# The opening of a hybrid attention step as one list by positions in the products: early loads of x, rows of x in other places, first roots on ScalarE and VectorE

## The chip, the cores and the metric

The kernel runs on one core of one Trainium2 chip. The metric is device time in microseconds (us) of one launch. The core has five engines with queues of their own: TensorE (PE), VectorE (DVE), ScalarE (ACT), GpSimd (POOL) and SyncE (SP), which here issues the DMAs. They meet through semaphores.

## The reference

One layer of a streaming encoder for a prompt of 1024 tokens (8 blocks of 128) and a sample of 64 tokens that shares the weights. Cut to what matters here:

```python
h = rms_norm(x, g)
p = h @ w_in                         # [q_A k_A v_A | q_B k_B v_B | forget logits]
qa, ka = rms_norm(heads(q_A), g_qa), rms_norm(heads(k_A), g_ka)
logf = log_sigmoid(f_logit + b_f)
# attention A: chunks of 64 frames see themselves and 8 chunks before, 8 heads of 64
logits = q @ k.T * scale + rel_bias
o = softmax(where(mask, logits, -inf)) @ v
# attention B: forgetting attention, 8 heads; then
x += concat(o_A, o_B) @ w_o          # then memory cross-attention and a conv FFN
```

## The kernel before

The projection and the attention run in eight head pairs (p = 0 to 7; 0 to 3 are attention A). A pair takes its 384 columns of the weights (392 in the first, which has the forget columns too) and forms the product of each token block t with them into one PSUM bank, `pj`. All operands are split into a high and a low part (`whi`, `wlo`, `xhi`, `xlo`), and a product has three terms for each of eight k: 24 matmuls, in 8 *pieces* of three. x comes from memory transposed, in columns of 256 tokens (columns 0 to 3, each in two halves of four k); ACT makes the high part and DVE the low one. The rows of x (`xn`, a block of 128 tokens) are loaded a second time untransposed, to form each token's mean square on ACT (`stats`).

This case is about the *opening*, the first pair. The products of t = 0 to 3 are formed together while weights and x still arrive (`quad`, banks `tq`, `O` and two of `PT`); then t = 4 to 7 one by one; then the product of the sample's 64 tokens (`proj_sample`, 16 matmuls). Beside them runs the attention of the pair, in steps:

- `E(t)`: evicts a product from PSUM (copy of q and k, squares, values, forget column `flog`).
- `QA(n)`: for blocks 2n and 2n+1, ACT squares and copies, DVE reduces the squares (L369), adds a constant (L370), and POOL takes the power −1/2 (L371).
- `Z(t)`: norm of q and k: POOL multiplies by the roots (L375 for t < 4; `qk_norm` with L296 to L310 after that), DVE splits the values (L397, L398).
- `R(t)`: the *turn*: PE transposes q and k of four heads (L405) into bank `tq`, ACT makes `kh` and `q` (L319), DVE `kl` and the low half of `q` (L320).
- `U(n, j)`: scores of one head (unit n = 2 · group + head; a group is two blocks, j the block in it): matmuls into `S` (L578), DVE adds the bias and takes the row maximum (L581), ACT the exponential with its sum (L583), DVE the reciprocal (L584), POOL scales (L586). `S` is one tile of two banks.
- `V(n)`: values: PE transposes the weights of attention into `PT` (L618), ACT and DVE split them (`pth`, `ptl`, L619 and L620), PE sums (L633).

A list `opening[t]` holds the steps beside product t, and `weave` spreads them evenly between its pieces. Until the end of t = 5 all engines keep the order of the code (`ramp` marks it, and `in_order` adds the dependencies); after that a scheduler may change it, but for the splits. Units 5 to 7, and the turn of block 7, are left to the second pair.

```python
def weave(main, subs):
    j = 0
    for x, f in enumerate(main):
        f()
        while j * len(main) < len(subs) * (x + 1):
            subs[j]()
            j += 1
```

Of the kernel before, what the change touches and what calls it, by code (L numbers as in the profile page):

```python
# [41 lines left out]
def hybrid_step(ctx: ExitStack, tc: tile.TileContext, i: dict, o: dict):  # L42
# [76 lines left out]
    xs = xp.tile([P, KT, 2, S], F32R, name="xs")  # L119
# [16 lines left out]
    def split_x(hi, lo, raw, k):  # L136
        act.activation(hi, raw, ACT.Copy, scale=gcol[:, 0, k:k + 1])
        dve.scalar_tensor_tensor(lo, raw, gcol[:, 0, k:k + 1], f32(hi), op0=ALU.mult, op1=ALU.subtract)
# [12 lines left out]
    def load_stats(t):  # L151
        rows = P if t < NT else S
        xn = xns[t] = wk.tile([P, N], F32, name="s", bufs=4)
        nc.sync.dma_start(xn[:rows, :D], i["xn"][t * P:t * P + rows])
# [25 lines left out]
    def split_col(c, k, raw):  # L180
# [3 lines left out]
        split_x(*[x_part(a, k, c * 256, 256) for a in range(2)], raw, k)  # L184
# [4 lines left out]
    def sample_columns(raw):  # L189
# [4 lines left out]
        def split():  # L194
            act.copy(xs[:, :, 0], raw)
            dve.tensor_tensor(xs[:, :, 1], raw, f32(xs[:, :, 0]), op=ALU.subtract)
# [12 lines left out]
    for k in range(KT):  # L209
# [31 lines left out]
    def stats4():  # L241
        st = bank("pj")[:, :8].rearrange("p (t z) -> p t z", z=2)
        for t in range(4):
            pe.matmul(st[:, t], quads[0][:, 0, t * P:t * P + P], two, start=True, stop=True)
        ms = wk.tile([P, 9], F32, name="ms1", bufs=2)
        dve.tensor_scalar(ms[:, :4], st[:, :, 0], EPS, None, op0=ALU.add)
        rsq(wk, ms[:, :4], rstd1[:, 0:4], 4)
        dve.tensor_scalar(eps1[:, 0:4], ms[:, :4], EPS, None, op0=ALU.mult)

# [107 lines left out]
    sq4, raw4, r8 = [], [], {}  # L357

    def quad_norm(n):
        if not n:  # L360
            for x in (sq4, raw4):
                x.append(wk.tile([P, N], F32, name="s", bufs=4)[:, :1024].rearrange("p (t c) -> p t c", t=4))
        for t in range(2 * n, 2 * n + 2):
            act.activation(sq4[0][:, t], quad[t][:, 0:256], ACT.Square, scale=0.125)
            act.copy(raw4[0][:, t], quad[t][:, 0:256])
        m = wa.tile([P, 2, 4], F32, name="m8", bufs=2)
        r = r8[n] = wa.tile([P, 2, 4], F32, name="r8", bufs=2)
        c = slice(2 * n, 2 * n + 2)
        dve.tensor_reduce(m.rearrange("p t h -> p (t h)"), sq4[0][:, c].rearrange("p t (h d) -> p (t h) d", h=4), axis=AX.X, op=ALU.add)  # L369
        dve.tensor_tensor(m, m, eps1[:, c].rearrange("p (t o) -> p t o", o=1).broadcast_to([P, 2, 4]), op=ALU.add)  # L370
        pool.tensor_tensor(r, m, mhalf[:, 0:4].rearrange("p (o h) -> p o h", o=1).broadcast_to([P, 2, 4]), op=ALU.pow)  # L371

    def quad_qk(t):
# [3 lines left out]
        return qk, None  # L377

    def proj(p, t, pj, first=False):
# [4 lines left out]
        if not first:  # L384
            raw = wa.tile([P, 256], F32, name="qkraw", bufs=2)
            act.copy(raw, pj[:, 0:256])
            sq = squares(pj[:, 0:256], P)
        vf = wa.tile([P, 2, 64], F32, name="vf", bufs=2)
        act.activation(vf.rearrange("p h d -> p (h d)"), pj[:, 256:384], ACT.Copy, scale=rstd1[:, t:t + 1])
        if p == 0:  # L390
            dve.scalar_tensor_tensor(flog[:, t], pj[:, 384:392], rstd1[:, t:t + 1], bfb, op0=ALU.mult, op1=ALU.add)
# [1667 lines left out]
```

## Time and profile before

| | |
|---|---|
| median of 3 runs | 1751.9 us (1751.48 to 1755.92) |
| the profiled execution | 1751.61 us, span 1749.8 us |
| mean granted clock of PE | 0.995 |
| PE busy | 1700.0 us, 97% of the span |
| from 20 to 40 us | PE busy 15.84 of 20 us, clock 1.00 |
| from 40 to 60 us | PE busy 14.60 of 20 us, clock 0.83 |
| from 60 to 80 us | PE busy 16.27 of 20 us, clock 0.74 |
| from 80 to 100 us | PE busy 17.25 of 20 us, clock 1.00 |

The profile is of one execution. Busy time counts instructions that run; PE's matmuls are pipelined, so that a busy PE is not always PE at its peak. In a row of the timeline the first number is the start, the second the length, and the bracket at its end holds the idle time ahead of it on that engine and the instruction that ended it. In a row of waits stand the sum, the count and the longest. In a row of a group stand the busy time, the mean of one in ns, and the idle time ahead.

### The profile page before, as it was taken

How to read it: one execution, taken by the hardware profiler on the slowest of the kernel's cores; microseconds unless marked ns; L12 is line 12 of the kernel's file. 1: busy time of each engine (PE TensorE's matmuls, PEld its weight loads, DVE VectorE, ACT ScalarE, POOL GpSimd, SP SyncE). 2: the span in 40 equal slices, each digit the busy share in tenths (PEclk: the TensorE clock that was granted, in tenths of full speed). 3: DMA queues.
4: the chain of work that ended last, by engine and by line, in shares of the span. 5: the costliest groups of instructions: out<-in, count | busy, mean ns of one | idle time of the engine just before them, and what ended most of it. 6: DMA issues, size and time to landing. Idle time of an engine off the chain costs nothing.

```text
span 1749.8 us, 33690 instructions
## 1 busy us (share of the span) xinstructions
PE 1700.0 (97%) x12384; PEld 1653.9 (95%) x12384; DVE 1187.9 (68%) x2610; ACT 920.5 (53%) x2027; POOL 592.3 (34%) x874
## 2 busy tenths in 40 slices
PE   8898999999999999999999999999999999999999
PEld 7788999999998888999999999999999999999999
DVE  6778667677677755334444389777777777659996
ACT  6656667677677657334555455333334343434442
POOL 2646557779777302543443521000000000000000
PEclk9899999999999999999999999999999999999999
DMA  6222122222232677531112752222222222793332
GB/s 209 75 53 61 52 76 67 62 74 59 63 104 91 195 226 224 172 114 39 49 49 80 208 182 80 95 83 75 75 74 75 75 75 75 267 331 120 113 105 88
DMA packets 135156, 191.97 MB, mean 110 GB/s; under 512 B 23288, under 2 KB 78200, under 8 KB 134992
## 3 DMA queue, kind: packets, MB, share of 16 engines
q1 hardware_dynamic: 134992, 189.83, 34.6%
q8 instruction: 97, 1.59, 0.4%
q14 instruction: 67, 0.55, 0.1%
HBM read 148.01 MB, written 43.34 MB: 109 GB/s over the span
## 4 chain that ended last, share of the span: by engine, by line
PE 46%; DVE 5%; issue 2%; ACT 1%; POOL 1%; DMA 1%; SPq 0%; DVEq 0%; ACTq 0%; POOLq 0%
PE W L1614 26%; PE W L1938 10%; PE pj L1068 7%; PE S L1357 1%; PE tq L1393 1%; PE O L1393 1%; POOL lo L1050 1%; DVE f L1479 1%; PE PT L1380 0%; DVE lo L1479 0%; DVE lo L1050 0%; ACT hi L1478 0%; PE O L1357 0%; DMA f<-x2d 0%; DMA raw<-in_w_down_dram 0%
## 5 line engine op out<-in xcount | busy, mean ns | idle before, releaser
L353 PE MATMUL pj<-whi,xhi 128*128 128x384 f32 (+1 forms) x480 | 181.8, 379 | 0.4 <-ACT whi L131 0.4
L353 PE MATMUL pj<-wlo,xhi 128*128 128x384 f32 (+1 forms) x480 | 164.5, 343 | 5.4 <-POOL wlo L133 4.3
L353 PE MATMUL pj<-whi,xlo 128*128 128x384 f32 (+1 forms) x480 | 163.1, 340 | 0.0
L1614 PE MATMUL W<-h,hi 128*128 128x272 f32 x704 | 134.3, 288 | 1.4 <-ACT qlo L1750 1.4
L583 ACT ACTIVATE s<-s,mx 128x640 f32<-128x640 f32 (+7 forms) x128 | 94.3, 737 | 71.0 <-DVE mx L581 70.1
L1720 POOL COPY s<-gp 128x2 f32<-128x2 f32 x22 | 15.8, 719 | 336.1 <-DVE gp L1719 336.1
L1938 PE MATMUL W<-f,hi 128*128 128x272 f32 x672 | 127.5, 287 | 0.0
L620 DVE TENSOR_TENSOR ptl<-PT,pth 128x512 fp32r<-128x512 f32 (+2 forms) x192 | 99.4, 521 | 35.0 <-ACT pth L619 33.3
L1614 PEld LDWEIGHTS W<-h,hi 128*128 128x128 f32 x704 | 110.3, 188 | 1.7 <-ACT qlo L1750 1.6
L619 ACT CAST pth<-PT 128x512 fp32r<-128x512 f32 (+2 forms) x192 | 85.0, 450 | 40.7 <-PE PT L618 38.9
L1938 PEld LDWEIGHTS W<-f,hi 128*128 128x128 f32 x672 | 105.3, 188 | 0.3 <-DVE f L1479 0.2
L1614 PE MATMUL W<-h,lo 128*128 128x272 f32 x352 | 101.3, 288 | 0.0
L353 PEld LDWEIGHTS pj<-wlo,xhi 128*128 128x128 f32 x480 | 92.3, 192 | 6.7 <-POOL wlo L133 5.3
L1938 PE MATMUL W<-f,lo 128*128 128x272 f32 x336 | 96.8, 288 | 0.2 <-DVE lo L1479 0.2
L1478 ACT CAST hi<-raw 128x512 fp32r<-128x512 f32 x68 | 42.2, 621 | 102.4 <-PE W L1614 59.2
L618 PE MATMUL PT<-ident,s 128*128 128x128 f32 x528 | 89.8, 277 | 5.7 <-DVE ptl L620 3.9
L353 PEld LDWEIGHTS pj<-whi,xhi 128*128 128x128 f32 x480 | 92.3, 192 | 1.2 <-ACT whi L131 0.5
L586 POOL TENSOR_SCALAR s<-s,ssum 128x640 f32<-128x640 f32 (+6 forms) x96 | 71.2, 742 | 63.0 <-DVE ssum L584 42.7
L353 PEld LDWEIGHTS pj<-whi,xlo 128*128 128x128 f32 x480 | 91.0, 190 | 0.0
L1068 PE MATMUL pj<-a,hi 128*128 128x384 f32 (+1 forms) x352 | 87.8, 333 | 1.5 <-DVE a L1121 1.3
L578 PE MATMUL S<-kh,q 128*128 128x256 f32 (+1 forms) x304 | 76.9, 278 | 10.7 <-DVE mx L581 10.7
L618 PEld LDWEIGHTS PT<-ident,s 128*128 128x128 f32 x528 | 65.8, 141 | 15.9 <-DVE ptl L620 9.1
(585 smaller groups left out, 5952.2 us busy)
## 6 DMA issues: line engine op xcount, KB each, us to landing
raw<-in_w_down_dram SPq DMA_DIRECT2D x45, 256.0 KB, 3.0
wraw<-in_w_dram SPq DMA_DIRECT2D x56, 192.0 KB, 2.5
raw<-in_w_up_dram SPq DMA_DIRECT2D x41, 256.0 KB, 2.8
h<-ad SPq DMA_DIRECT2D x32, 272.0 KB, 5.4
mwraw<-in_w_mkv_dram SPq DMA_DIRECT2D x16, 512.0 KB, 5.1
raw<-in_w_mo_dram SPq DMA_DIRECT2D x32, 256.0 KB, 3.2
kvraw<-in_w_down_dram SPq DMA_DIRECT2D x32, 256.0 KB, 3.4
ad<-t SPq DMA_DIRECT2D x22, 272.0 KB, 2.1
```

The lines of the kernel that those rows point to most:

```text
L353: pe.matmul(pj[:, :nw], x_part(a, k, t * P, P), wt[k][b][:, :nw], start=n == 0, stop=n == 3 * KT - 1)
L578: pe.matmul(sp[:, a:a + (k1 - k0) * P], q, kk[:, h, src], start=m == 0, stop=m == 1)
L583: act.activation(s[:, :n], s[:, :n], ACT.Exp, bias=mx, scale=-1.0, accum_out=sm)
L586: pool.tensor_scalar(s[:, :n], s[:, :n], sm, 1.0, op0=ALU.mult, op1=ALU.mult)
L618: pe.transpose(pt[:, b - ch[0]], self.s[j][:, (b - w0) * P:(b - w0 + 1) * P], ident)
L619: act.copy(hi[:, f:f + n, j], pt[:, f:f + n])
L620: dve.tensor_tensor(lo[:, f:f + n, j], pt[:, f:f + n], f32(hi[:, f:f + n, j]), op=ALU.subtract)
L1068: pe.matmul(out()[:, :cn], w[a][:, k % 4], x[b][k][:, c0:c0 + cn], start=k == 0 and (a, b) == SPLIT[0], stop=k == KT - 1 and (a, b) == SPL ...
L1393: pe.matmul(op[:, a0:a1], v[x][:, b, d * P:(d + 1) * P], self.p2[y][:, b, a0:a1], start=n == 0, stop=n == 5)
L1478: act.copy(hi, t)
L1614: pe.matmul(w[:, z, :Q], a(p, j), rights[j][b][:, z * Q:z * Q + Q], start=fresh and begin and j == 0 and x == 0, stop=final and end and j ...
L1938: pe.matmul(ws[m][:, z, :Q], la[p][:, m * P:(m + 1) * P], ra[b][:, z * Q:z * Q + Q], start=first and y == 0 and what in opening, stop=fina ...
```

## The change

- All four columns of x are asked for at the start, and the rows of blocks 4 to 7 early; rows 4 lie in the place of the sample's x, rows 5 and 6 in those of `pth` and `ptl`. The small loads (forget bias, gains) come behind x.
- Of column 3, the high parts of k = 0 to 3 are made on POOL, those of k = 4 to 7 on ACT.
- The roots for blocks 0 to 3 are taken by Ln and Exp on ACT and three DVE operations (`quad_rsq`), not by POOL's power.
- `early_v` splits the values of blocks 0 to 3 from PSUM; `evict` copies all 392 columns of later blocks at once, and squares and values are made from the copy. The statistics of blocks 4 to 7 are ended together.
- `U(n, j)` scores two heads, n and n + 1, one in each bank of one `S` tile. Turns of t < 4 alternate between banks `tq` and `O`.
- `opening[t]` is a list of (position, step), and `place` runs a step behind the piece with that number. All engines but SP keep the order of the code until the sample's product has been issued.

In the diff, `qk_norm` stands at L348 to L365 now, `place` at L393.

```diff
             nc.sync.dma_start(gcol, i["gcol"].rearrange("n p k -> p n k"))
+    load_stats(4, "xs")
+    xraws = {c: [load_x(c, z) for z in range(2)] for c in (2, 3)}
     nc.sync.dma_start(bfb, i["b_f"].broadcast_to([P, 8]))
     for d in range(2):
         nc.sync.dma_start(gd[d * 64:(d + 1) * 64], i["gqkT"])
+    load_rows(0)
     for kind in range(2):
         nc.sync.dma_start(gk[:, kind], i["gqk"][kind, 1:2].broadcast_to([P, 64]))
-    xraws = {2: [load_x(2, z) for z in range(2)]}
-    load_rows(0)
...
+    def quad_mean(n):
+        m = m8[n] = wa.tile([P, 2, 4], F32, name="m8", bufs=2)
+        c = slice(2 * n, 2 * n + 2)
+        dve.tensor_reduce(m.rearrange("p t h -> p (t h)"), sq4[0][:, c].rearrange("p t (h d) -> p (t h) d", h=4), axis=AX.X, op=ALU.add)
+        dve.tensor_tensor(m, m, eps1[:, c].rearrange("p (t o) -> p t o", o=1).broadcast_to([P, 2, 4]), op=ALU.add)
+
+    def quad_rsq(n):
+        m = m8[n].rearrange("p t h -> p (t h)")
+        r8[n] = wa.tile([P, 2, 4], F32, name="r8", bufs=2)
+        y = wa.tile([P, 8], F32, name="y8")
+        a = wa.tile([P, 8], F32, name="a8")
+        act.activation(y, m, ACT.Ln)
+        act.activation(y, y, ACT.Exp, scale=-0.5)
+        dve.tensor_tensor(a, m, y, op=ALU.mult)
+        dve.scalar_tensor_tensor(a, a, -0.5, y, op0=ALU.mult, op1=ALU.mult)
+        dve.scalar_tensor_tensor(r8[n].rearrange("p t h -> p (t h)"), a, 1.5, y, op0=ALU.add, op1=ALU.mult)
 
...
-    for f in columns(2, 0, xraws[2][0]):
+    x2a, x2b = columns(2, 0, xraws[2][0]), columns(2, 1, xraws[2][1])
+    for f in x2a:
         f()
+    load_stats(7)
+    stats(4)
     for t in range(4):
         for a, b in TERMS:
             quad_mm(KT - 1, t, a, b)
         if t == 0:
-            stats4()
-    for f in columns(2, 1, xraws[2][1]):
+            stats4(0)
+            quad_ev(0)
+            stats4(1)
+        if t == 1:
+            quad_ev(1)
+    for f in x2b[:2]:
+        f()
+    quad_mean(0)
+    quad_rsq(0)
+    for f in x2b[2:]:
         f()
...
+        def early_v(self):
+            t = self.t
+            g, j = self.group()
+            src = quad[t][:, 256:384].rearrange("p (h d) -> p h d", h=2)
+            act.activation(g.v[:, j, :, 0], src, ACT.Copy, scale=rstd1[:, t:t + 1])
+            dve.scalar_tensor_tensor(g.v[:, j, :, 1], src, rstd1[:, t:t + 1], f32(g.v[:, j, :, 0]), op0=ALU.mult, op1=ALU.subtract)
+            dve.scalar_tensor_tensor(flog[:, t], quad[t][:, 384:392], rstd1[:, t:t + 1], bfb, op0=ALU.mult, op1=ALU.add)
+
+        def early_qk(self):
+            self.qk = quad_qk(self.t)
+
+        def evict(self, pj):
+            self.raw = wa.tile([P, 392], F32, name="qkraw", bufs=2)
+            act.copy(self.raw, pj[:, :392])
+
+        def parts(self):
+            t = self.t
+            self.sq = squares(self.raw[:, 0:256], P)
+            self.vf = wa.tile([P, 2, 64], F32, name="vf", bufs=2)
+            act.activation(self.vf.rearrange("p h d -> p (h d)"), self.raw[:, 256:384], ACT.Copy, scale=rstd1[:, t:t + 1])
+            dve.scalar_tensor_tensor(flog[:, t], self.raw[:, 384:392], rstd1[:, t:t + 1], bfb, op0=ALU.mult, op1=ALU.add)
+
+        def norm(self):
+            t = self.t
+            g, j = self.group()
+            self.qk, self.k = qk_norm(0, self.sq, self.raw, eps1[:, t:t + 1], P)
+            dve.tensor_copy(g.v[:, j, :, 0], self.vf)
+            dve.tensor_tensor(g.v[:, j, :, 1], self.vf, f32(g.v[:, j, :, 0]), op=ALU.subtract)
...
-            sp = ps.tile([P, 2, 512], F32, name="S", bufs=1).rearrange("p a b -> p (a b)")
+            if sp is None:
+                sp = ps.tile([P, 2, 512], F32, name="S", bufs=1).rearrange("p a b -> p (a b)")
...
+    for u in units:
+        u.s = {}
+    mains = {}
+    blocks = [Block(t, ("tq", "O")[t % 2] if t < 4 else "tq") for t in range(NT)]
...
     def U(n, j):
+        def both():
+            sp = ps.tile([P, 2, 512], F32, name="S", bufs=1)
+            for h in range(2):
+                units[n + h].score(j, sp[:, h])
+        return both
...
     opening = {
-        4: QA(0) + E(0) + E(1) + [scale_gain, lambda: load_bias(0)] + Z(0) + QA(1) + Z(1) + [lambda: load_x3(0), lambda: load_x3(1)]
-           + E(2) + E(3) + R(0) + L(4),
-        5: R(1) + U(0, 0) + Z(2) + Z(3) + U(0, 1) + L(5) + split_x3(0) + R(2) + norms(4, 5) + E(4) + U(1, 0),
-        6: split_x3(1) + R(3) + V(0) + U(1, 1) + Z(4) + L(6) + U(2, 0) + E(5) + norms(6),
-        7: V(1) + L(7) + [lambda: xsraw.append(load_x(4, 0))] + U(2, 1) + R(4) + Z(5) + norms(7) + U(3, 0) + E(6) + split_xs(),
-        8: V(2) + U(3, 1) + R(5) + Z(6) + U(4, 0) + E(7) + V(3) + U(4, 1) + norms(8) + R(6)}
-    units[4].s = {}
+        4: [(-1, lambda: load_stats(5, "pth")), (-1, lambda: load_stats(6, "ptl")), (-1, lambda: load_bias(0)),
+            (0, B[0].early_qk), (0, B[1].early_qk), (0, lambda: quad_ev(2)), (0, lambda: quad_ev(3)), (1, scale_gain), (1, B[0].early_v),
+            (3, lambda: stats(7)), (4, B[0].turn), (5, lambda: quad_mean(1)), (5, lambda: quad_rsq(1)), (6, B[1].early_v), (7, B[1].turn)],
+        5: [(0, lambda: B[4].evict(mains[4])), (0, x3(0, pool)), (0, x3(1, pool)), (1, U(0, 0)), (1, B[2].early_qk), (1, B[3].early_qk),
+            (2, x3(4)), (2, x3(5)), (3, lambda: stats(5)), (4, U(0, 1)), (4, B[2].early_v), (5, B[2].turn), (5, x3(6)), (5, x3(7)),
+            (6, x3(2, pool)), (6, x3(3, pool)), (6, B[3].early_v), (7, lambda: stats(6)), (7, lambda: stats_end(4, 8)), (7, B[3].turn)],
+        6: [(0, lambda: B[5].evict(mains[5])), (0, V[0][0]), (0, V[0][1]), (1, B[4].parts), (2, V[1][0]), (2, V[1][1]), (2, B[4].norm),
+            (3, V[0][2]), (4, U(2, 0)), (4, B[5].parts), (5, V[1][2]), (5, B[5].norm), (6, U(2, 1)), (7, B[4].turn)],
+        7: [(0, lambda: B[6].evict(mains[6])), (1, V[2][0]), (2, V[2][1]), (2, lambda: xsraw.append(load_x(4, 0))), (2, B[6].parts),
+            (3, V[3][0]), (3, B[5].turn), (3, lambda: load_stats(8)), (4, V[3][1]), (4, B[6].norm), (5, V[2][2]), (6, sample_split[0]), (6, sample_split[1]),
+            (7, V[3][2])],
+        8: [(0, lambda: B[7].evict(mains[7])), (0, lambda: units[4].score(0)), (2, B[7].parts), (3, B[6].turn), (4, lambda: units[4].score(1)),
+            (5, lambda: stats(8)), (5, lambda: stats_end(8, 9))]}
     for p, np_ in zip(PAIRS, PAIRS[1:] + (None,)):
...
                 subs = opening[t]
+                for at, f in subs:
+                    if at < 0:
+                        f()
...
-            weave(main, subs)
             if p:
+                weave(main, subs)
                 turns.append(proj(p, t, pj))
             else:
+                place(main, subs)
...
-            if p == 0 and t == 5:
-                ramp.append(len(nc.cur_bb.bb.instructions))
...
-            turns.append((lambda: norm_of[7](), lambda: turn_of[7]()))
+            turns.append((B[7].norm, B[7].turn))
         turns.append(proj_sample(p, subs))
+        if p == 0:
+            ramp.append(len(nc.cur_bb.bb.instructions))
```

Three places in the program, as rows of an engine with the semaphores that they wait for.

DVE, from the end of the first turn's preparations to the first score maximum. Names: `flog` forget column, `m`, `a`, `r` the reduce and the root, `kl`, `q` the turn. Before:

```order
L369 TENSOR_REDUCE m_443<-s 128x8 [waits Activation_49]
L370 TENSOR_TENSOR m_443<-m_443,eps_82 128x8 [waits DVE_49]
L397 CAST v<-vf 128x2x64
L398 TENSOR_TENSOR v<-vf,v 128x2x64 [waits DVE_49]
L391 SCALAR_TENSOR_TENSOR flog<-PT,rstd_81,bfb 128x8 [waits PE_49,Activation_49] x2
L320 SCALAR_TENSOR_TENSOR kl<-tq,gd,kh 128x2x128 [waits PE_49,Activation_49]
L320 SCALAR_TENSOR_TENSOR q<-tq,gd,q 64x2x128
L320 SCALAR_TENSOR_TENSOR kl<-tq,gd,kh 128x2x128 [waits PE_49,Activation_49]
L320 SCALAR_TENSOR_TENSOR q<-tq,gd,q 64x2x128
L581 ISA s,mx<-S,bias 128x128 [waits DMAHW4_49,DMAHW3_49,PE_49]
```

The same stretch now:

```order
L375 SCALAR_TENSOR_TENSOR kl<-tq,gd,kh 128x2x128 [waits PE_49,Activation_49]
L375 SCALAR_TENSOR_TENSOR q<-tq,gd,q 64x2x128 [waits DVE_49]
L280 TENSOR_REDUCE m_475<-s 128x8
L281 TENSOR_TENSOR m_475<-m_475,eps_82 128x8 [waits DVE_49]
L290 TENSOR_TENSOR a_480<-m_475,y_479 128x8 [waits DVE_49,Activation_49]
L291 SCALAR_TENSOR_TENSOR a_480<-a_480,y_479 128x8 [waits DVE_49]
L292 SCALAR_TENSOR_TENSOR r_478<-a_480,y_479 128x8 [waits DVE_49]
L434 SCALAR_TENSOR_TENSOR v<-O,rstd_81,v 128x2x64 [waits Activation_49]
L435 SCALAR_TENSOR_TENSOR flog<-O,rstd_81,bfb 128x8
L375 SCALAR_TENSOR_TENSOR kl<-O,gd,kh 128x2x128 [waits PE_49,Activation_49]
L375 SCALAR_TENSOR_TENSOR q<-O,gd,q 64x2x128
L145 SCALAR_TENSOR_TENSOR xlo<-pth,gcol,xhi 128x256 [waits DMAHW4_49,Pool_49]
```

The reduce and root of blocks 2 and 3 and the forget column of block 1 stood ahead of the first turn's `kl`, and stand behind it now.

PE at the first scores (`S<-kh,q` and `S<-kl,q` are one head's). Before:

```order
L405 MATMUL tq<-ident,qk 128x128 x3
L578 MATMUL S<-kh,q 128x128
L578 MATMUL S<-kl,q 128x128
L353 MATMUL pj<-whi,xhi 128x392
L353 MATMUL pj<-wlo,xhi 128x392
```

And now:

```order
L670 MATMUL S<-kh,q 128x128 [waits Activation_49]
L670 MATMUL S<-kl,q 128x128
L670 MATMUL S<-kh,q 128x128 [waits DVE_49]
L670 MATMUL S<-kl,q 128x128
L408 MATMUL pj<-whi,xhi 128x392
L408 MATMUL pj<-wlo,xhi 128x392
```

The second head follows the first with no product between them; the DVE instruction that its first matmul waits for is the first head's maximum (L673).

POOL ahead of the sample's product (`s<-s,gcol` multiplies the sample's x by the gain). Before:

```order
L296 TENSOR_SCALAR m<-m,eps_82 128x4 [waits DVE_49]
L297 TENSOR_TENSOR r<-m,mhalf 128x4 [waits Pool_49]
L133 TENSOR_TENSOR wlo<-wraw,whi 128x384 [waits DMAHW3_49,Activation_49]
L133 TENSOR_TENSOR wlo<-wraw,whi 128x384 [waits DMAHW4_49,Activation_49]
L298 TENSOR_TENSOR qk<-qkraw,r 128x512 [waits PE_49,Pool_49]
L310 TENSOR_TENSOR ko<-qk,gk 128x128 [waits DMAHW2_49,Pool_49]
L192 TENSOR_TENSOR s<-s,gcol 128x512 [waits DMAHW6_49]
L586 TENSOR_SCALAR s<-s,ssum 128x512 [waits DVE_49]
```

And now:

```order
L678 TENSOR_SCALAR s<-s,ssum 128x512 [waits DVE_49,PE_49] x2
L137 TENSOR_TENSOR wlo<-wraw,whi 128x384 [waits DMAHW6_49,Activation_49]
L137 TENSOR_TENSOR wlo<-wraw,whi 128x384 [waits DMAHW7_49,Activation_49]
L351 TENSOR_SCALAR m<-m,eps_82 128x4 [waits DVE_49]
L352 TENSOR_TENSOR r<-m,mhalf 128x4 [waits Pool_49]
L353 TENSOR_TENSOR qk<-qkraw,r 128x512 [waits PE_49,Activation_49,Pool_49]
L365 TENSOR_TENSOR ko<-qk,gk 128x128 [waits DMAHW3_49,Pool_49]
L205 TENSOR_TENSOR s<-s,gcol 128x512 [waits DMAHW7_49,PE_49]
```

The gain stood behind block 5's norm and ahead of the softmax scalings; it stands behind block 6's norm now, and behind those scalings.

More of the change, by code (lines that the diff above doesn't have):

```diff
@@ L183, in split_col @@
                 x2.setdefault((a, c), []).append(quarter_tile(part, f"x{part}"))
[L184 removed]
+        split_x(*[x_part(a, k, c * 256, 256) for a in range(2)], raw, k, e)
     def columns(c, z, raw):
@@ L355, in products @@
         return pj, pieces(3 * KT, 3, one)
[L357 to L371, printed above, removed]
     def quad_qk(t):
@@ L383, in proj @@
         j = t % 2
[L384 to L387, printed above, removed]
+        raw = wa.tile([P, 392], F32, name="qkraw", bufs=2)[:, :256]
+        act.copy(raw, pj[:, 0:256])
+        sq = squares(pj[:, 0:256], P)
         vf = wa.tile([P, 2, 64], F32, name="vf", bufs=2)
         act.activation(vf.rearrange("p h d -> p (h d)"), pj[:, 256:384], ACT.Copy, scale=rstd1[:, t:t + 1])
-        if p == 0:
-            dve.scalar_tensor_tensor(flog[:, t], pj[:, 384:392], rstd1[:, t:t + 1], bfb, op0=ALU.mult, op1=ALU.add)
         qk = kflat = None
```

109 lines of the change are left out of this document (66 added, 43 removed).

## The prediction

> **What bounds the kernel now.** I read the page's busy shares, then the windows of the opening, the waits of PE there, PE's timeline, and last the groups of instructions by shape, for prices.
>
> ```profile
> PE 1700.0 (97%) x12384; PEld 1653.9 (95%) x12384; DVE 1187.9 (68%) x2610; ACT 920.5 (53%) x2027; POOL 592.3 (34%) x874
> ```
>
> PE is busy in 97% of the span, so only what PE loses can be won. The change touches the opening alone: it begins to differ at about 21 us and ends with the sample product at about 77 us. The windows show that stretch as one of the few where PE has much to lose (columns: window, length, busy time and count of PE, PEld, DVE, ACT, POOL, then PEclk, DMA share, GB/s):
>
> ```profile
> 27.00:43.00 16.00, 10.12 (x61) 8.42 (x59) 10.42 (x37) 8.30 (x24) 8.60 (x8) 1.00 0.35 118
> 43.00:72.00 29.00, 21.78 (x100) 20.26 (x101) 19.90 (x64) 19.19 (x59) 17.43 (x23) 0.71 0.31 91
> ```
>
> PE idles 5.9 of the first 16 us at full clock; in the next 29 it runs at a granted clock of 0.71. No engine is full. These are waits along a chain that goes from engine to engine, as PE's waits from 27 to 78 us say:
>
> ```profile
> PE S L578 <- DVE mx L581: 3.5, 2, 2.5
> PE O L633 <- ACT pth L619: 3.2, 2, 3.0
> PE tq L405 <- POOL qk L375: 3.1, 3, 1.7
> PE PT L618 <- POOL s L586: 1.6, 1, 1.6
> PE tq L405 <- DVE q L320: 1.4, 1, 1.4
> PE O L633 <- DVE ptl L620: 0.4, 1, 0.4
> ```
>
> They add to 13.2 us. PE's timeline shows what a long one costs beyond itself:
>
> ```profile
> 27.24 0.34 PE L353 MATMUL pj<-whi,xhi 128*128 128x392 f32 x1
> 27.42 0.34 PE L353 MATMUL pj<-wlo,xhi 128*128 128x392 f32 x1
> ...
> 30.17 0.66 PE L405 MATMUL tq<-ident,qk 128*128 128x128 f32 x4 [1.69 <-POOL qk L375]
> 30.58 0.43 PE L353 MATMUL pj<-whi,xhi 128*128 128x392 f32 x1
> ...
> 32.96 0.63 PE L405 MATMUL tq<-ident,qk 128*128 128x128 f32 x4 [1.06 <-POOL qk L375]
> ...
> 45.76 0.58 PE L633 MATMUL O<-pth,v 128*128 128x256 f32 x1 [3.04 <-ACT pth L619]
> ...
> 61.97 0.58 PE L578 MATMUL S<-kh,q 128*128 128x256 f32 x1 [2.45 <-DVE mx L581]
> ...
> 63.97 0.53 PE L353 MATMUL pj<-whi,xhi 128*128 128x392 f32 x1
> 64.30 0.53 PE L353 MATMUL pj<-wlo,xhi 128*128 128x392 f32 x1
> ...
> 77.34 0.60 PE L405 MATMUL tq<-ident,qk 128*128 128x128 f32 x4
> ```
>
> Matmuls of one product start 0.18 us apart (27.24, 27.42), and 0.33 apart after the stall of 2.45 us: half clock. After 1.69 and 1.06 the clock held at 1.00. How much that costs: from 24.5, where t=4 begins (15 matmuls ahead of 27.24), to 77.75, behind the last turn, lie 53.2 us, 40.0 of them without a wait. In them PE issues 96 product and 16 sample matmuls (0.18 each, 20.2), 48 transposes (0.10 each, four from 30.17 to 30.58; 4.9) and 60 smaller ones of scores and sums of values (an estimate by their width against 392 columns: 0.12 at most, 7.2). That is 32, so 8 us more are lost. I put 2 of them down to ten stalls at which a matmul (0.34) drains before the next can start, instead of 0.18, and 6 to half clock behind 45.76 and 61.97. So the opening loses 13.2 + 8 = 21 us; this is the most that any reordering can win.
>
> **The change part by part.** Prices first: the groups by line and shape from 20 to 80 us that the sum uses, of three engines (mean ns of one behind the comma):
>
> ```profile
> L371 POOL TENSOR_TENSOR r<-m,mhalf 128x8 f32<-128x8 f32 x2 | 3.3, 1647 | 26.1 <-DVE m L370 26.0
> L297 POOL TENSOR_TENSOR r<-m,mhalf 128x4 f32<-128x4 f32 x4 | 4.1, 1030 | 0.3
> L298 POOL TENSOR_TENSOR qk<-qkraw,r 128x512 f32<-128x512 f32 x4 | 4.2, 1043 | 0.2
> L310 POOL TENSOR_TENSOR ko<-qk,gk 128x128 f32<-128x128 f32 x4 | 1.9, 478 | 0.3
> L296 POOL TENSOR_SCALAR m<-m,eps 128x4 f32<-128x4 f32 x4 | 1.3, 319 | 12.2 <-DVE m L293 12.2
> L586 POOL TENSOR_SCALAR s<-s,ssum 128x256 f32<-128x256 f32 x2 | 1.1, 566 | 0.0
> L192 POOL TENSOR_TENSOR s<-s,gcol 128x512 f32<-128x512 f32 x1 | 1.0, 1042 | 0.0
> L138 DVE SCALAR_TENSOR_TENSOR xlo<-pth,gcol,xhi 128x256 fp32r<-128x256 f32 x8 | 3.8, 534 | 0.2 <-ACT xhi L137 0.2
> L320 DVE SCALAR_TENSOR_TENSOR kl<-tq,gd,kh 128x256 fp32r<-128x256 f32 x7 | 3.4, 482 | 3.2 <-ACT q L319 2.8 <-ACT kh L319 0.2
> L293 DVE TENSOR_REDUCE m<-sq 128x4 f32<-128x256 f32 x4 | 1.6, 412 | 0.1
> L369 DVE TENSOR_REDUCE m<-s 128x8 f32<-128x512 f32 x2 | 1.4, 682 | 0.2 <-ACT s L364 0.2
> L581 DVE CUSTOM_DVE_ANT_0 s<-S,bias 128x128 f32<-128x128 f32 x2 | 0.6, 288 | 0.0
> L196 DVE TENSOR_TENSOR xs<-s,xs 128x512 fp32r<-128x512 f32 x1 | 1.0, 1021 | 0.0
> L319 ACT ACTIVATE kh<-tq,gd 128x256 fp32r<-128x256 f32 x7 | 3.3, 465 | 1.9 <-PE tq L405 1.8
> L76 ACT ACTIVATE rsq_y<-ms 128x4 f32<-128x4 f32 x1 | 0.2, 206 | 2.2 <-DVE ms L246 2.2
> L78 DVE TENSOR_TENSOR rsq_a<-ms,rsq_y 128x4 f32<-128x4 f32 x1 | 0.2, 164 | 0.5 <-ACT rsq_y L77 0.5
> ```
>
> *Loads.* The third column of x and the rows of x (blocks 4 to 7) are asked for some 10 to 30 us earlier, the small gains and biases behind them. I price this at nothing:
>
> ```profile
> 32.00:36.00 4.00, 1.00 0.00 0
> ```
>
> The queue moves nothing from 32 to 36 us, so the load can go forward; the latest tile then is the second half of the bias, needed at about 38 us. If it came late, PE would wait at the first scores: bounds 0 and 1 us.
>
> *Roots.* Two POOL powers (1.65 each) become an Ln and an Exp (0.21 each, 0.4 in all) and three DVE steps (0.16 each, 0.5): 0.7 us shorter each, and POOL loses 3.3 us. *Splits:* four high parts of x3 go from ACT to POOL; the nearest POOL row with that width is 0.57, so 2.3 us; POOL has them done before products need them. *Values* of blocks 0 to 3 skip a cast; *evictions* copy 392 columns instead of 256; the statistics of blocks 4 to 7 end once instead of three times: together 1 to 3 us of DVE and ACT work that lies beside PE, priced at nothing on the path.
>
> *The fixed order* sets the result: now all four compute engines run every step where the list puts it. I walked the list with the rows above.
>
> First turn. PE meets it behind piece 4 of t=4, at 27.24. The new root ends near 27.7 and its POOL product (1.04, as L298) near 28.8, but the turn takes over the bank of quad product 0 and so also needs that block's forget column. This stands on ACT behind Exp (26.9), two x splits (0.4 each) and four evictions of blocks 2 and 3 (start to start 0.26), and a value copy: 29.1, then two DVE steps: 29.7. Stall 2.5 (before: 1.69).
>
> Second turn. Ready transposes at 30.6, kh and q on ACT 0.8, kl and q on DVE 1.0: 32.5. Only then, in DVE's order, the reduce for blocks 2 and 3 (0.7), the sum, the root (1.0) and block 1's values (0.5): 34.8. PE is there at 31.9. Stall 2.9, and the turn comes 1.8 us later than the 32.96 of before.
>
> Score pairs. Each step U now scores two heads into two halves of one tile, and the second head's first matmul waits for the first head's maximum. In the first pair that maximum stands on DVE behind kl and q of block 1 and two low parts of x3 (34.8 + 0.8 + 0.8 + 1.0 + 0.8, and 0.37 itself = 38.6), while PE stands there from 36.5: 2.1. By the same addition U(0,1) has PE at 40.7 and its maximum, behind two low parts and two reciprocals, at 42.1: 1.5; U(2,0) 52.9 and 53.9: 1.0; U(2,1) 56.2 and, behind a sum's mix, a reduce and two value steps, 58.8: 2.6.
>
> Values. The second transposes of V(0, 1) need block 3's forget column, behind some ten DVE steps (PE at 45.4, column at 48.0): 2.5. V3 waits twice for its low part: 1.3 and 0.8.
>
> Sample. Its split needs POOL's gain, which stands behind block 6's norm. That norm's reduce stands on DVE behind block 5's turn (PE 64.5, then 0.8 + 0.8 + 1.0) and a low part: 68.1. Then POOL 0.32 + 1.03 + 1.04 + 0.48 = 71.0, gain 72.0, and the copy (0.6) and difference (1.02): 73.7. PE is there at 69.7. Stall 4.0.
>
> The new waits add to 2.5 + 2.9 + 7.2 + 2.5 + 2.1 + 4.0 = 21.2, against 13.2: +8. Neither list leaves other work to the pairs behind.
>
> *Clock and drains.* Before lost 8 us here. Eleven new stalls drain for 2 us as ten did. Of the new stalls only the last is clearly longer than the 2.45 that was enough before; 2.5, 2.9, 2.5 and 2.6 are near it. But while PE's next wait is for another engine, a slow matmul only shortens that wait. I take 2 us behind the last stall, with nothing left to wait for (16 products at 0.15 more), and nothing ahead of it: 4 in place of 8. Bounds for half clock: 0 and 9 (five stretches of 12 matmuls at 0.15, 1.8 each).
>
> [...]
>
> *Behind the opening.* In the second pair PE waits for splits of its weights (PE's waits from 78 to 92 us):
>
> ```profile
> PE pj L353 <- DVE wlo L133: 1.1, 1, 1.1
> PE pj L353 <- POOL wlo L133: 0.8, 1, 0.8
> PE pj L353 <- ACT whi L131: 0.4, 1, 0.4
> ```
>
> Together 2.3 us. ACT, DVE and POOL reach this place with less left over when PE comes later, so up to 2.3 of a delay is absorbed; they stand behind the sample product in program order, so it could be 0. I take 2.
>
> Sum: +8 − 4 − 2 = +2 on 1751.61 (the profiled execution, 1.8 us more than its span of 1749.8, 0.3 below the median of the runs): 1753.6, and 1754 on the median.
>
> **The rivals.**
>
> *Queues shorter than added (faster).* My addition runs DVE as a full queue, but the window from 43 us shows it busy 19.9 of 29. If the forced order lets DVE and ACT start steps as I have them but without the tenths that I add where one engine hands to the next, only both turns and the first two pairs bind (9.0), the sample waits 1: 10, against 13.2, and no stretch falls to half clock: −3.2 − 6 = −9, 1743. For it: POOL is 3.3 us lighter and x's parts are ready early. Against it: each named step is behind others on an in-order engine. It decides at the sample: if block 6's reduce ends before about 65, the stall is gone.
>
> *Half clock after each stall near 2.5 (slower).* Five stretches at 1.8 us, one third hidden by later waits, cost 6 like before's two, and half as much is absorbed behind the opening: +8 + 0 − 1 = +7, 1759. For it: the row of 61.97; the first two stalls decide it, at 29.8 and 34.8. Against it: the 13.2 us of waits before include two such stretches only, and 1.69 did none.
>
> *The second pair swallows it (no change).* If the weight splits set the pace of the second pair whatever the opening does, the end does not move: 1752. For it, three waits that end at three engines; against it, they are 2.3 us in all, and a gain or loss above that shows.
>
> **How the numbers follow.** The forecast has 0.34 (its own range 1748 to 1759), the faster rival 0.26, half clock 0.30, the swallowed one 0.10. 0.3%, or 5.3 us, is about what can be told from no change: below 1746.6 faster, above 1757.2 slower. Of the forecast 0.25 lies within, 0.07 above, 0.02 below; of the faster rival 0.21 below, 0.05 within; of half clock 0.20 above, 0.10 within; the last is within. So faster 0.23, same 0.50, slower 0.27. The range runs from 1742 to 1763: both rivals, with up to 4 us above the slower one (five stretches with nothing hidden, a late load) and 1 below the faster, and 0.2 left out.
>
> **What would show it.** Right: PE's first turn at about 29.8 and second at 34.8, each pair's second head waiting 1 to 2.6 us for the first head's maximum, a stall of about 4 us ahead of the sample product named after its low part, the opening's last PE instruction at 80 to 82 instead of 77.3. Wrong: a granted clock of 1.00 from 43 to 72 with those waits under 1 us (faster), clock below 0.7 from 28 to 60 (slower), or a start of the sample product before 70. A prediction that is wrong most likely fails in the DVE queue: I add each step at its mean duration, and a few tenths per step over 60 steps shift every stall.

## The result, and the profile after

The changed kernel takes 1762.52 us (median of 4 runs, 1760.76 to 1764.18) against 1752.26 before: ratio 1.0054, interval [1.0037, 1.0072]. It is 10.3 us slower. The profiled execution took 1762.22 us, its span is 1760.4.

The same windows as before, of the changed kernel (window, length, then busy time and count of PE, PEld, DVE, ACT, POOL, PEclk, DMA share, GB/s):

```profile
27.00:43.00 16.00, 8.31 (x41) 7.32 (x39) 9.63 (x33) 8.31 (x25) 4.62 (x7) 0.89 0.48 150
43.00:72.00 29.00, 21.36 (x122) 19.89 (x123) 18.21 (x59) 17.67 (x50) 13.83 (x20) 0.88 0.17 45
72.00:84.00 12.00, 7.89 (x35) 7.33 (x35) 4.61 (x13) 4.09 (x10) 6.73 (x9) 0.72 0.22 59
```

POOL is lighter (4.62 of 16 us, before 8.60) and PE does less in the first window (8.31 against 10.12). The slow clock is spread over all three windows. The waits of PE from 24 to 86 us:

```profile
PE S L670 <- DVE mx L673: 5.5, 4, 2.3
PE pj L517 <- DVE xs L211: 3.7, 1, 3.7
PE tq L465 <- POOL xhi L144: 3.4, 1, 3.4
PE O L465 <- DVE flog L435: 3.0, 1, 3.0
PE PT L710 <- DVE ms L179: 2.5, 1, 2.5
PE PT L710 <- DVE ptl L712: 1.0, 1, 1.0
PE O L725 <- DVE mix L735: 0.4, 1, 0.4
```

They add to 19.5 us against 13.2 before. The third and the fifth name the wrong releaser: the first turn starts at 30.74, right behind the forget column of block 0 on DVE, the transposes of V(0, 1) at 50.35, behind that of block 3 (DVE's timeline):

```profile
29.87 0.33 DVE L760 TENSOR_SCALAR gd<-gd 128x2 f32<-128x2 f32 x1
30.12 0.34 DVE L434 SCALAR_TENSOR_TENSOR v<-tq,rstd,v 128x128 fp32r<-128x128 f32 x1
30.38 0.21 DVE L435 SCALAR_TENSOR_TENSOR flog<-tq,rstd,bfb 128x8 f32<-128x8 f32 x1
...
49.99 0.22 DVE L435 SCALAR_TENSOR_TENSOR flog<-PT,rstd,bfb 128x8 f32<-128x8 f32 x1
```

PE's timeline:

```profile
30.74 0.63 PE L465 MATMUL tq<-ident,qk 128*128 128x128 f32 x4 [3.37 <-POOL xhi L144]
...
35.95 1.07 PE L465 MATMUL O<-ident,qk 128*128 128x128 f32 x4 [2.98 <-DVE flog L435]
...
50.35 0.41 PE L710 MATMUL PT<-ident,s 128*128 128x128 f32 x2 [2.50 <-DVE ms L179]
...
62.70 0.39 PE L670 MATMUL S<-kh,q 128*128 128x256 f32 x1 [2.25 <-DVE mx L673]
...
78.44 0.69 PE L517 MATMUL pj<-whi,xs 128*128 128x392 f32 x1 [3.69 <-DVE xs L211]
78.94 0.53 PE L517 MATMUL pj<-wlo,xs 128*128 128x392 f32 x1
79.26 0.53 PE L517 MATMUL pj<-whi,xs 128*128 128x392 f32 x1
...
85.64 0.34 PE L408 MATMUL pj<-whi,xhi 128*128 128x384 f32 x1
...
99.46 0.45 PE L408 MATMUL pj<-wlo,xhi 128*128 128x384 f32 x1 [2.00 <-POOL wlo L137]
...
102.92 0.52 PE L408 MATMUL pj<-whi,xhi 128*128 128x384 f32 x1
103.24 0.52 PE L408 MATMUL pj<-wlo,xhi 128*128 128x384 f32 x1
```

The last four rows belong to the second pair: its first product, its longest wait for a split of its weights, and two products at half clock (0.32 us apart; the granted clock from 101 to 104 is 0.50). In the kernel before the first product stands at 78.55 and the longest wait for a split ends at 90.18 (1.07 us). To follow the difference further I take one step of each pair, the DVE sum that ends the eviction of the sample's product (`sm`). In the trace of before it stands at 78.96 in the first pair and at 159.33 in the second, in the changed one at 92.31 and 169.25:

| | before | after | difference |
|---|---|---|---|
| first product of the second pair | 78.55 | 85.64 | +7.1 |
| from there to the sample of the second pair | 80.8 | 83.6 | +2.8 |
| from there to the end of the span | 1590.5 | 1591.2 | +0.7 |

So two thirds are lost in the opening and most of the rest in the second pair, whose own steps the change does not touch. The opening's +7.1 are +6.2 of waits and +0.9 of clock and drains: from 24.5 us to 85.64 PE is without a wait for 41.7 us, before for 40.8.

What the second pair meets is on ACT (timeline, changed kernel):

```profile
87.19 0.83 ACT L675 ACTIVATE s<-s,mx 128x640 f32<-128x640 f32 x1 [1.92 <-DVE mx L673]
87.93 0.19 ACT L675 ACTIVATION_READ_ACCUMULATOR s<-s,mx 128x1 f32 x1
88.02 1.04 ACT L174 ACTIVATE s<-s 64x1024 f32<-64x1024 f32 x1
...
90.69 0.48 ACT L521 COPY sm<-pj 64x392 f32<-64x392 f32 x1
```

The copy of the sample's product, ready at about 86, runs at 90.69: in the fixed order it stands behind a score's exponential, the statistics of block 8 (88.02) and their root. Before, the scheduler ran it at 77.54, right behind the last sample matmul.

The waits are the smaller part of the +2.8. In the second pair PE is busy for 74.8 us in the changed kernel and for 72.7 before, at a mean granted clock of 0.98 and 1.00: 2.1 us come from there, since half clock follows the wait that ends at 99.46, and 0.7 are idle time of PE. On POOL the split that PE waits for stands behind the norm of the sample (its product starts at 97.18, the split at 98.42); before, that norm was done at 85.99, ahead of POOL's two splits (86.73).

### The profile page after: what moved, and what is told of

The parts are those of the page before. It is cut to its first block, busy times and chain, and to the rows that moved or that the text cites. A ratio compares the mean times of both kernels' runs of the same rounds, so it can differ in the third digit from the quotient of the medians.

```text
span 1760.4 us, 33674 instructions
## 1 busy us (share of the span) xinstructions
PE 1702.7 (97%) x12384; PEld 1655.9 (94%) x12384; DVE 1185.4 (67%) x2602; ACT 919.6 (52%) x2023; POOL 591.5 (34%) x876
## 4 chain that ended last, share of the span: by engine, by line
PE 48%; DVE 4%; issue 1%; POOL 1%; ACT 1%; DMA 0%; ACTq 0%; DVEq 0%; POOLq 0%
PE W L1695 25%; PE W L2019 10%; PE pj L1149 7%; PE W L1149 2%; PE S L1438 1%; PE tq L1474 1%; PE O L1474 1%; POOL lo L1131 1%; DVE f L1560 1%; PE PT L1461 0%; DVE lo L1560 0%; ACT hi L1559 0%; PE O L1438 0%; DMA raw<-in_w_down_dram 0%; PE PT L1419 0%
```

## The experiments

All but the changed kernel itself were timed in five rounds beside the kernel before, whose median in them was 1752.7 to 1753.8, so I compare ratios. The columns: time over that of before with its interval; start of the second pair's first product; how much later than that the first pair's sum of the sample comes; the second pair's length as above (all in us); and PE's mean granted clock in it. All but the ratio are of one profiled execution each, which can lie 2 us off the median (combined: 1750.16 against 1752.48); and what follows the second pair takes 1589.8 to 1593.4 us, though no edit touches it.

| kernel | ratio | second pair starts | sample's sum | second pair | clock in it |
|---|---|---|---|---|---|
| before | 1 | 78.55 | +0.4 | 80.8 | 1.00 |
| after | 1.0054 [1.0037, 1.0072] | 85.64 | +6.7 | 83.6 | 0.98 |
| values_first | 1.0035 [1.0022, 1.0049] | 79.55 | +6.7 | 83.6 | 0.98 |
| scores_apart | 1.0057 [1.0044, 1.0069] | 84.58 | +6.7 | 84.1 | 0.98 |
| sample_early | 1.0018 [1.0010, 1.0027] | 78.45 | +7.0 | 85.1 | 0.96 |
| all_three | 1.0027 [1.0016, 1.0037] | 81.41 | +6.7 | 83.8 | 0.98 |
| stats8_early | 1.0044 [1.0031, 1.0057] | 84.35 | +5.0 | 82.8 | 1.00 |
| short_order | 0.9988 [0.9979, 0.9997] | 76.04 | +1.4 | 80.9 | 1.00 |
| combined | 0.9997 [0.9988, 1.0005] | 75.32 | +5.9 | 83.3 | 1.00 |
| before_roots | 1.0015 [1.0006, 1.0024] | 80.41 | +0.4 | 80.8 | 1.00 |
| combined_short | 0.9956 [0.9943, 0.9968] | 71.99 | +1.8 | 81.3 | 1.00 |
| order_t7 | 1.0014 [1.0005, 1.0023] | 81.33 | +0.7 | 79.6 | 1.00 |
| filled_wait | 1.0051 [1.0038, 1.0065] | 81.86 | +7.0 | 85.1 | 0.96 |
| before_loads | 0.9991 [0.9982, 1.0000] | 75.42 | +0.4 | 81.5 | 0.98 |

### Three places of the list, one by one and together

Values and forget columns first:

```diff
-(-1, lambda: load_bias(0)), ... (0, lambda: quad_ev(2)), (0, lambda: quad_ev(3)), (1, scale_gain), (1, B[0].early_v), ... (6, B[1].early_v)
+(0, B[0].early_v), (0, B[1].early_v), (0, lambda: quad_ev(2)), (0, lambda: quad_ev(3)), (1, lambda: load_bias(0)), (1, scale_gain)
```

> Only the places of steps at t=4 change: the values and forget columns of blocks 0 and 1 stand on ACT and DVE ahead of the evictions of blocks 2 and 3, the bias load with its four fills and the gain behind them. Theory A (each late step costs its own wait and the slow clock behind it): the first turn at about 29.8 us instead of 30.74, the second at about 32 instead of 35.95 with no stall, no half clock at 36 to 39; the opening ends 4 to 5 us earlier, 1757 to 1759 us. Theory B (DVE and ACT in order are the bound, a wait that goes comes back at the next step): the score pairs wait longer by what the turns gain; under 1.5 us won, 1761 to 1763.

Measured 1759.35 us, 3.3 us less than the changed kernel by the ratios. The first turn starts at 29.48 (wait 2.48) and is followed by half clock (30.0 to 33.1, products 0.33 us apart), the second does not wait, and no slow clock follows it; the opening ends 6.1 us earlier. The first pair of scores waits 1.94 instead of 0.91: a part comes back, as theory B has it. The time lies between the two forecasts. Of the 6.1 us only 3.3 arrive in it; the profiled execution (1757.64) is the fastest of the five, and what follows the second pair took 1.5 us more in it than in the changed kernel.

Scores of a pair apart:

```diff
-(1, U(0, 0)), ... (4, U(0, 1)), ... (4, U(2, 0)), ... (6, U(2, 1))
+(1, U1(0, 0)), ... (3, U1(1, 0)), ... (4, U1(0, 1)), ... (6, U1(1, 1)), ... (3, U1(2, 0)), (5, U1(3, 0)), (6, U1(2, 1)), and U1(3, 1) at piece 0 of t=7
```

> Only the score steps change: each of the eight scores is a step of its own with its own S tile, one or two pieces behind the other head of its pair. Theory A: the 5.5 us that PE waits for the first head's maximum (0.9 + 1.7 + 0.7 + 2.3) fall to about 1.5, 1758 to 1760 us. Theory B: the second scores come later, so their exponentials and scalings do, and V waits for them: under 1.5 us won, 1761 to 1763.

Nothing won: 1763.72 us, 0.7 above theory B's range. The waits of this kernel say why:

```profile
PE PT L710 <- DVE flog L435: 3.9, 1, 3.9
...
PE S L670 <- DVE mx L673: 2.5, 3, 1.5
```

The scores wait 2.5 us instead of 5.5, and the transposes of V, which waited 2.5 us for block 3's forget column, wait 3.9. For the pairs theory B holds: the maximum was not the cause but the place at which DVE's queue was met.

The sample's gain and split ahead of block 6's norm:

```diff
-(4, V[3][1]), (4, B[6].norm), (5, V[2][2]), (6, sample_split[0]), (6, sample_split[1]),
+(4, sample_split[0]), (4, V[3][1]), (4, sample_split[1]), (4, B[6].norm), (5, V[2][2]),
```

> Only the sample's gain on POOL and its split move ahead of block 6's norm. Theory A: the stall of 3.69 us ahead of the sample product goes, and with it the half clock from 78 to 84 (14 matmuls at 0.15, some 2 us and more with the scores there): the opening ends 5 to 6 us earlier, 1756 to 1758 us. Theory B: the norm of block 6 comes 2 us later and the second pair waits for it and for its weight splits: 1 to 3 us won, 1759 to 1761.

1756.83 us, as theory A had it. The stall of 3.69 us and the slow clock behind it are gone, and the opening ends at 78.45, where it ended before. And yet the kernel is 0.18% slower than before: this is what turned me to the second pair, which takes 85.1 us here, 3.2 of the 4.3 more than before as busy time of PE: the wait of 2.00 us for the split stands here too (92.57), with half clock behind it (the granted clock from 90 to 100 is 0.66).

> The three moves together. Theory A: the gains add, 12 to 15 us: 1747 to 1751 us, below the kernel before. Theory B: they overlap, 4 to 7 us: 1755 to 1758, still above it.

1758.62 us, above both forecasts and worse than the sample's move alone. The moves do not add here: one by one they won 3.3, −0.5 and 6.3 us by the ratios, together 4.7. V waits 3.8 us for block 3's forget column and its sum 2.9 us for a DVE sum (`mix`) that now stands behind the sample's difference and block 6's reduce.

### How far the order is fixed

Statistics of block 8 at piece 1:

```diff
+(1, lambda: stats(8)), (1, lambda: stats_end(8, 9)), (2, B[7].parts), (3, B[6].turn), (4, lambda: units[4].score(1))]
-(5, lambda: stats(8)), (5, lambda: stats_end(8, 9))]
```

> The changed kernel with one move: the statistics of block 8 stand at piece 1 of the sample product, not at piece 5. The second pair's part up to its sample product took 83.6 us in the changed kernel against 80.8 before (from its first product). Theory C: this comes from the sample's eviction, which the fixed order holds on ACT behind these statistics (90.69 us, 5 us behind the last sample matmul; before 1.5), so that the sample's norm on POOL falls among the weight splits; the move brings back 2 to 3 us: 1759 to 1760.5. Theory D: the splits are late whatever the statistics do: 1762 to 1763.

1760.47 us, inside theory C's range, but the trace does not bear the theory out in full: the sample's sum still comes 5.0 us late, and only 0.8 us of the gain lie in the second pair. The statistics are one of the steps in front of the eviction, not the only one.

The order of the code kept to the end of t=5, as before:

```diff
+            if p == 0 and t == 5:
+                ramp.append(len(nc.cur_bb.bb.instructions))
...
-        if p == 0:
-            ramp.append(len(nc.cur_bb.bb.instructions))
```

> The changed kernel with its list, but all engines keep the order of the code only to the end of t=5, as before; behind that the scheduler may choose. Theory C (forced places cost: the sample's gain, its eviction, the third column's splits): 4 to 8 us won, 1755 to 1759. Theory D (the list's places cost whoever orders the rest): under 2 us won, 1760.5 to 1763.

1750.47 us: 11.6 us less than the changed kernel by the ratios, more than either theory gave it, and 0.12% faster than before, with the list and all else of the change in place. The first two stalls (3.39 and 2.97 us) are still there; what goes is behind them. PE's waits from 24 to 86 us:

```profile
PE tq L465 <- POOL xhi L144: 3.4, 1, 3.4
PE O L465 <- DVE flog L435: 3.0, 1, 3.0
PE pj L517 <- DVE xs L211: 2.7, 1, 2.7
...
PE S L670 <- DVE mx L673: 1.8, 2, 1.7
```

The score pairs wait 1.8 us (5.5), V does not wait for a forget column, and the sample's sum comes 1.4 us behind the second pair's first product (6.7). The order to the end of t=7 tells the two halves apart:

```diff
+            if p == 0 and t == 7:
+                ramp.append(len(nc.cur_bb.bb.instructions))
```

> The changed kernel with its list; the fixed order ends with t=7 instead of with the sample's product. Theory E: the waits to 75 us stay as they are, the sample's stall may stay, but its eviction goes at once and the second pair takes 81 us instead of 83.6: 1758.5 to 1760.5 us; the other 8 us of the short order's gain then lie between t=5 and t=7. If the hold on the sample's part is the larger share: 1752 to 1756.

1756.09 us: I had the shares wrong. 7.0 us by the ratios come from freeing the sample's part alone; 4.6 more lie between t=5 and t=7. The opening ends 4.3 us earlier and the second pair is 4.0 shorter, 2.9 of it as busy time of PE at full clock instead of 0.98; what follows took 2.2 us more. On ACT the eviction now stands where the product ends:

```profile
81.53 0.48 ACT L521 COPY sm<-pj 64x392 f32<-64x392 f32 x1 [2.20 <-PE pj L517]
```

The scheduler also filled the sample's stall: it ran block 6's turn and two scores ahead of the sample product, and the wait fell to 1.77.

### Parts of the change on the kernel before

Roots by Ln and Exp:

```diff
-        pool.tensor_tensor(r, m, mhalf ..., op=ALU.pow)
+        act.activation(y, mf, ACT.Ln)
+        act.activation(y, y, ACT.Exp, scale=-0.5)
+        dve.tensor_tensor(a, mf, y, op=ALU.mult)
+        dve.scalar_tensor_tensor(a, a, -0.5, y, op0=ALU.mult, op1=ALU.mult)
+        dve.scalar_tensor_tensor(r, a, 1.5, y, op0=ALU.add, op1=ALU.mult)
```

> The kernel before with one part of the change: the roots of blocks 0 to 3 by Ln and Exp on ACT and three DVE steps. If the root was on the path, POOL's product starts 0.7 us earlier, the first stall (1.69) falls to about 1.0 and the second by as much: 1 to 2 us won. If another engine gives it back: within 1 us of before.

Neither forecast: 0.15% slower. The first turn does come 0.7 us earlier, as the root is shorter by that. The second comes 2.6 us later:

```profile
29.49 0.66 PE L412 MATMUL tq<-ident,qk 128*128 128x128 f32 x4 [1.21 <-POOL qk L382]
...
35.55 0.83 PE L412 MATMUL tq<-ident,qk 128*128 128x128 f32 x4 [4.33 <-DVE q L320]
```

The first turn's `kh` on ACT and `kl` on DVE stand in order behind the second root and what waits for it (`kh` at 33.55, before 30.96; `kl` at 34.41, before 31.82), and the second turn needs their bank. The longer root on POOL stood in neither queue.

Column 3 of x at the start:

```diff
-    xraws = {2: [load_x(2, z) for z in range(2)]}
+    xraws = {c: [load_x(c, z) for z in range(2)] for c in (2, 3)}
```

> The kernel before with one part of the change: the third column of x is asked for at the start, behind the second. If the loads cost nothing and hide nothing: within 1 us of before. If the earlier bytes hold up the rows of x or the bias: 1 to 3 us slower.

1752.19 us against 1753.77, ratio 0.9991 with an interval that just touches 1: these loads cost nothing and may be worth a microsecond. (In the profiled execution, the fastest of its eleven, the opening ends 3.1 us earlier.) The earlier rows of x, the other part of the loads, were not tried alone.

### The clock

20 matmuls in the sample's stall:

```diff
+        if p == 0:
+            for _ in range(20):
+                pe.matmul(pj[:, :nw], x_part(0, 0, 7 * P, P), wt[0][0][:, :nw], start=True, stop=True)
```

> The changed kernel with 20 matmuls more on PE, into the sample's own bank ahead of its product, which starts the bank anew: they fill the 3.69 us in which PE waits. If the idle time lowers the clock, the sample product then runs at a spacing of 0.18 us and not 0.33: 1.5 to 2.5 us won, 1760 to 1761. If the clock falls for another reason, or the fill comes too late: 1762 to 1764.

```profile
73.16 3.73 PE L521 MATMUL pj<-whi,xhi 128*128 128x392 f32 x20
77.04 0.45 PE L517 MATMUL pj<-whi,xs 128*128 128x392 f32 x1 [0.15 <-DVE xs L211]
77.33 0.34 PE L517 MATMUL pj<-wlo,xs 128*128 128x392 f32 x1
77.50 0.34 PE L517 MATMUL pj<-whi,xs 128*128 128x392 f32 x1
```

The sample product runs at full clock, and the stretch from its first matmul to the second pair shrinks from 7.20 to 4.82 us. So here it was the idle time that lowered the clock (the stretch's products start 0.18 us apart now, 0.33 in the changed kernel), and the term is 2.4 us. The whole time did not follow (1762.50 us): it lies in the range of the other theory, though the rows speak against that theory's reasons. The wait for the weight split (1.99 us) is again followed by half clock (0.32 us apart), for longer than in the changed kernel (from 95.96 to about 102, there from 100.1 to about 104.4); the second pair takes 85.1 us and the rest 1593.2 (1591.2). Whether the slow stretch only moves, or this is the spread between runs, one profile cannot tell; it stays open.

### What combines

```diff
4: early_v of blocks 0 to 3 ahead of (or right behind) the evictions, load_bias and scale_gain behind them
4: (4, B[0].turn) -> (6, B[0].turn)
7: the sample's gain and split as in sample_early
8: the statistics as in stats8_early
```

> The changed kernel with four moves: values and forget columns of all four first blocks ahead of the evictions of blocks 2 and 3, the first turn at piece 6 instead of 4, the sample's gain and split ahead of block 6's norm, the statistics of block 8 at piece 1. If each wait is caused by its place, the first stall falls from 3.4 to under 1.5 us, the second and the one of 2.5 us at 47 us go, the one ahead of the sample too: the opening ends at 73 to 75 us (before 78.5), 1746 to 1750 us. If the DVE chain gives the waits back: 1753 to 1757.

1752.48 us, between the two forecasts, no different from before. The opening ends at 75.3 as hoped, 3.2 us ahead of before; the sample's sum 5.9 us late gives 2.5 of it back in the second pair. With the short order in addition:

> The kernel with four moved places (1752.5 us) and, in addition, the order of the code kept only to the end of t=5. Theory E (the fixed order behind t=5 costs about 12 us in the changed kernel; what is left of it in the one with four moves is the sample's eviction, 2.4 us in the second pair): opening ends at 73 to 75.5 us, second pair 81 instead of 83.3; 1747 to 1749.5 us, below before and below the one with the short order alone. If both mend the same waits: 1750 to 1752.

1745.66 us, ratio 0.9956 [0.9943, 0.9968]: faster than before by 8 us, than the changed kernel by 17, and 1.3 below the forecast. The opening ends at 72.0 and the second pair takes 81.3. PE's waits in it from 24 to 86 us:

```profile
PE PT L710 <- POOL s L678: 2.6, 1, 2.6
PE S L670 <- ACT qkraw L442: 2.3, 1, 2.3
PE pj L408 <- POOL wlo L137: 2.1, 1, 2.1
...
PE S L670 <- DVE mx L673: 0.8, 2, 0.5
```

## Why the prediction was right and where it was not

1762.52 lies at the upper edge of the range (1742 to 1763), inside it by half a microsecond and with one of the four runs (1764.18) outside: that it is inside is luck. The likeliest time, 1754, was 8.5 us too low, and "slower", which came, had 0.27. The case that came closest is the rival of half clock (1759), to which I gave 0.30 against 0.34 for my forecast; but its sign, a clock below 0.7 from 28 to 60, did not show (0.89). Of the signs for my own forecast the waits of the pairs and the sample's stall came, the end of the opening at 80 to 82 did not (85.5).

*The waits: right.* Forecast 21.2 us, measured 19.5. One by one, forecast and measured: first turn 2.5 and 3.37, second 2.9 and 2.98, pairs 2.1, 1.5, 1.0, 2.6 and 0.91, 1.65, 0.66, 2.25, V(0, 1) 2.5 and 2.50, V3 2.1 and 1.4 (close by luck: the two waits for V3's low part did not come, others did, for V1's low part and ahead of V3's sum), sample 4.0 and 3.69. The first turn came at 30.74 and not 29.8, since I left out the four fills of the bias and the gain, which stood on DVE ahead of block 0's values (29.24 to 30.1). The experiments confirm the causes of the turns and of the sample's stall. Of the pairs they do not: apart, the wait moved to V.

*Clock and drains: wrong by 5 us.* I let the changed kernel lose 4 us here where before lost 8; it lost 0.9 more than before. The step that failed is "nothing ahead of it": half clock followed the second turn (36.7 to 39 us), the values (53.5 to 56.4), the fourth pair (63.3 to 66.4) and the sample's wait: the granted clock is 0.50 from 37 to 38.5, 54 to 56, 65 to 66 and 81 to 83. I had argued that a slow matmul only shortens the next wait. The runs show both cases. filled_wait has the same code up to the sample's stall, and in its profile half clock follows the first turn (30.33); its second turn still comes at 36.00, against 35.95 in the changed kernel, so there the wait took it up. Behind the fourth pair it did so only in part: from there to the sample product pass 15.74 us in the changed kernel, at half clock, and 15.15 in filled_wait, at full clock. The reason that I see is that the engines which release PE wait for PE's transposes and scores too, so that a slow PE delays its own release; this is read from the order of the steps, no run shows it alone. The sample's share, 2 us by my sum, measured 2.4.

*Behind the opening: wrong by 5 us.* I took −2, it was +2.8. I had counted the work that is left, not its order. The fixed order ends behind the sample's part of the code, its eviction included, and I had read it only on the engines' rows up to the product. The table shows it: where the order is fixed through the sample the second pair takes 82.8 to 85.1 us in eight kernels, where it is not, 79.6 to 81.5 in six. order_t7, where only the end of the fixed order differs, goes from one group to the other. What the order does there is known in part. Of the +2.8 in the changed kernel 2.1 are time at a lower clock behind one wait of 2.00 us, a term that my sum did not have; short_order meets that wait (2.06) without half clock and takes 80.9. At full clock the fixed order still costs some 2 us (stats8_early 82.8, combined 83.3). That this is the lateness of the eviction alone, and not some other step of that part, is argued from the ACT rows, and whether the lower clock belongs to the order or to chance stays open.

Sum: +6.2 + 0.9 + 2.8 + 0.7 = +10.6 of the span, against +8 − 4 − 2 forecast.

*Priced parts.* Loads at nothing: shown for the third column of x, on the kernel before. The roots at a gain of 0.7 us each beside the path: the root is that much shorter, but on the kernel before it costs 2.3 us, for its steps stand in two queues on which the turns depend.

## What to carry to other kernels

An order that is fixed by hand should end where it has been read to its end: here a list that won 2 us with a short fixed order cost 10 with a long one, since it also held the sample's eviction, and scores and values, behind steps that did not need to come first. When work leaves a slow engine for a faster one, count what stands behind it in the new queue, not the saving (before_roots: a root 0.7 us shorter, the kernel 2.3 us slower). Before forecasting that a stall costs only itself, look whether the engines that end the next stall wait for PE too (here an explanation, not a measurement).

## What the runs showed of the hardware

*Which stall is followed by a lower clock changes from run to run.* In the profile of the changed kernel the first stall, 3.37 us, is followed by full clock (four transposes take 0.63), in that of sample_early, whose code is the same up to there, one of 3.15 by half clock (1.09):

```profile
30.29 1.09 PE L465 MATMUL tq<-ident,qk 128*128 128x128 f32 x4 [3.15 <-POOL xhi L144]
```

and in the changed kernel stalls of 2.25 us (62.70) and 2.00 us (99.46) were followed by it, while one of 2.06 us at the same split was not in short_order (PE; a product takes 0.34 us there, as at full clock):

```profile
84.42 0.44 PE L408 MATMUL pj<-wlo,xhi 128*128 128x384 f32 x1 [2.06 <-POOL wlo L137]
...
85.45 0.42 PE L408 MATMUL pj<-whi,xhi 128*128 128x384 f32 x1
85.71 0.34 PE L408 MATMUL pj<-wlo,xhi 128*128 128x384 f32 x1
```

So the length alone does not decide in these rows: in one profile full clock followed 3.37 us, and half clock 2.25 and 2.00. What decides besides it was not shown.

*DVE and POOL took longer side by side.* Two low parts of x took DVE 0.88 us where POOL was idle, and 1.66 us while POOL multiplied q and k by their roots, one of the two 1.26 instead of 0.48 (changed kernel, DVE and POOL):

```profile
22.55 0.88 DVE L145 SCALAR_TENSOR_TENSOR xlo<-pth,gcol,xhi 128x256 fp32r<-128x256 f32 x2
...
27.63 1.66 DVE L145 SCALAR_TENSOR_TENSOR xlo<-ptl,gcol,xhi 128x256 fp32r<-128x256 f32 x2
```

```profile
27.86 2.32 POOL L414 TENSOR_TENSOR qk<-s,r 128x512 f32<-128x512 f32 x2 [26.56 <-DVE r L292]
```

POOL's two multiplications took 1.14 and 1.22 us there, the four in the kernel before 1.04 to 1.09 each. In DVE's order the two low parts stand ahead of the first forget column, so some 0.8 us of its lateness (it ended at 30.6) are an estimate for this (1.66 less 0.88). By what one engine slows the other was not shown.
